# A decoder trunk's feed-forward scheme and rope: additions to h queued ahead of weight splits, and the queries' rotation in three operations

## The chip, the cores and the metric

One Trainium2 chip, of which the kernel uses one core. The time is that of one execution on the device in microseconds, the median of several executions. The profile is that of one execution; times in its rows count from the start of its span.

## The reference

A decoder trunk of two layers on 512 tokens of width 1024, all in float32. The first layer mixes with a state-space scan (Mamba-2), the second with latent attention whose keys and values come from one compressed projection; each layer ends with a gated feed-forward network (FFN) behind a depthwise convolution, and every residual sum is normalised.

```python
def conv_ffn(h, up, conv_w, conv_b, down):            # hidden width 2816
    u = causal_depthwise_conv(h @ up, conv_w, conv_b)
    g, val = jnp.split(u, 2, axis=-1)
    return (jax.nn.silu(g) * val) @ down

def apply_rope(x, cos, sin):                          # 64 per head, 8 heads
    x1, x2 = jnp.split(xf, 2, axis=-1)
    return jnp.concatenate([x1 * cos - x2 * sin, x2 * cos + x1 * sin], axis=-1)
...
    for i in range(DEPTH):
        mix = ssd_mixer(h, ...) if i < N_A_LAYERS else mla_attention(h, ...)
        h = layer_norm(DN_ALPHA * h + mix, ln_mix_g[i], ln_mix_b[i])
        ff = conv_ffn(h, ffn_up[i], ffn_conv_w[i], ffn_conv_b[i], ffn_down[i])
        h = layer_norm(DN_ALPHA * h + ff, ln_ffn_g[i], ln_ffn_b[i])
```

## The kernel before

**Precision.** Each float32 operand of a product is kept as two float32r parts, high and low, and each product is three matmuls (L154 to L156 in `mm_b`, L148 in `mm_a`): high by high, high by low, low by high.

**Weights.** `WStream` brings all weights in one sequence of tiles (128 x 1024 or less). For each tile there are four steps: SyncE issues the load into a staging buffer `wst` (three buffers), ACT casts it into the high part `wh` (L84), VectorE subtracts for the low part `wl` (L85), which frees the staging buffer for the next load, and TensorE uses the pair, after which the pair (six of them) is free again. ACT and VectorE together are called the split here. `ahead` splits as many tiles as buffers and a look-ahead of four allow; `get` calls it before each use, and the code calls it again where a product ends.

**The seven-product scheme.** Of the FFN's 22 rows of hidden channels the first 10 go through `down_pairs`: in place of eight block products (two token halves, two row parities, two output halves) it forms seven, of sums and differences of the operands. In order: a11, s1, s2 and s4 alternating, s3, a12, a22. Each has three weight tiles (1024, 1024 and 512 wide), and each works on two banks of PSUM: X[0] and X[1] (X), Y or Z. X is accumulated on in a11, s2, s3 and a22 (`start` is false after the first), so each time X must be added to h (`add`, L341, one operation for each bank) before the next product that uses it starts on that bank. The order of the additions in the code is X after a11, Y after s1, X and Y after s2/s4, X after s3, Z after a12, X after a22.

The operands on the weight side are sums too. Three buffers `rs` hold them: the first weights come by plain loads, s1's are made by an accumulating transfer that GpSimd issues (L57), s2's by VectorE's sum L78, s3's by VectorE's subtraction L81 into the staging buffer, a22's again by an accumulating transfer, which may start once L81 has read the sums.

**Who sets the order.** Engines work in order. The tile framework's scheduler fixes each engine's order when the kernel is built, from the order in the code and its own model of when operands are ready; SyncE's order alone is that of the code. `tc.issue_after(x)` puts what is issued inside it behind instruction x.

**Rope.** In the attention layer `rope` rotates 64 columns of each query head (four token tiles, 128 x 512 in PSUM, from `qr_tile`) and of the shared key (four tiles, 128 x 64, from `down`) into SBUF by six VectorE operations of half the width, L1029 to L1034. The rotated queries `qr` are transposed by TensorE (L1166), cast and split (`qrT`, L1170 and L1171) and used in the scores (L1183).

Of the kernel before, what the change touches and what calls it, by code (L numbers as in the profile page):

```python
# [9 lines left out]
F32 = mybir.dt.float32  # L10
# [4 lines left out]
ALU = mybir.AluOpType  # L15
# [3 lines left out]
P = 128  # L19
# [6 lines left out]
ALPHA = 4.0 ** 0.25  # L26
# [4 lines left out]
class WStream:  # L31
# [284 lines left out]
def down_pairs(k, ws, n, prs):  # L316

    nc = k.nc
    X, Y, Z = ([k.bank() for _ in range(2)] for _ in range(3))
    ni = (len(prs) + 1) // 2
    seen = set()

    def product(bs, op, p, i, start, stop):
        wh, wl = ws.get(i)
        ps = prs[2 * p:2 * p + 2]
        for t in range(2):
            for q, pr in enumerate(ps):  # L330
                x, c0 = pr[op]
                sl = slice(q * 512, (q + 1) * 512)
                k.mm_b(bs[t], x, slice(c0 + t * P, c0 + (t + 1) * P), wh[:, sl], wl[:, sl],
                       start and p == 0 and q == 0, stop and p == ni - 1 and q == len(ps) - 1)
        ws.retire(i)

    def add(bs, row, hf, sign):
        for t in range(2):
            i = 2 * row + t
            hs = k.h[:, i, hf * 512:(hf + 1) * 512]  # L340
            nc.vector.scalar_tensor_tensor(hs, hs, 1.0 if (i, hf) in seen else ALPHA, bs[t], op0=ALU.mult,  # L341
                                           op1=ALU.add if sign > 0 else ALU.subtract)
            seen.add((i, hf))

    for p in range(ni):
        product(X, "a11", p, n + p, True, True)
    n += ni
    ws.ahead(n)
    add(X, 0, 0, 1)
    for p in range(ni):  # L350
        product(Y, "s1", p, n + p, True, True)
    n += ni
    ws.ahead(n)
    add(Y, 1, 1, 1)
    for p in range(ni):
        product(X, "s2", p, n + 2 * p, False, True)
        product(Y, "s4", p, n + 2 * p + 1, False, True)
    n += 2 * ni
    ws.ahead(n)
    add(X, 0, 1, -1)  # L360
    add(Y, 0, 1, 1)
    for bs, op, s0, out in ((X, "s3", False, (1, 1, -1)), (Z, "a12", True, (0, 0, 1)), (X, "a22", False, (1, 0, 1))):
        for p in range(ni):
            product(bs, op, p, n + p, s0, True)
        n += ni
        ws.ahead(n)
        add(bs, *out)
    return n


def ffn(k, ws, base, cwp, gb, la=2, out=None, mid=None):

    nc, tc = k.nc, k.tc
    with ExitStack() as c:
# [10 lines left out]
        for r in range(2):  # L385
# [582 lines left out]
AH, QR, KVR, RD = 8, 384, 256, 64  # L968
# [49 lines left out]
    k.cs = cs  # L1018


def rope(k, dst, ps, i, nh, tmp):

    nc = k.nc
    cos = k.cs[:, 0, i, :].unsqueeze(1).broadcast_to([P, nh, 32])
    sin = k.cs[:, 1, i, :].unsqueeze(1).broadcast_to([P, nh, 32])
    x1, x2 = ps[:, :, 0:32], ps[:, :, 32:64]
    d1, d2 = dst[:, :, 0:32], dst[:, :, 32:64]
    t = tmp[:, :, 0:32]
    nc.vector.tensor_tensor(d1, x1, cos, op=ALU.mult)  # L1029
    nc.vector.tensor_tensor(t, x2, sin, op=ALU.mult)  # L1030
    nc.vector.tensor_tensor(d1, d1, t, op=ALU.subtract)
    nc.vector.tensor_tensor(d2, x2, cos, op=ALU.mult)
    nc.vector.tensor_tensor(t, x1, sin, op=ALU.mult)
    nc.vector.tensor_tensor(d2, d2, t, op=ALU.add)  # L1034


def mla(k, ws, base, ngp, gb):
    nc, tc = k.nc, k.tc
    with ExitStack() as cx:
        pool = lambda n, b, **kw: cx.enter_context(tc.tile_pool(name=n, bufs=b, **kw))  # L1040
        one = pool("a1", 1)
# [17 lines left out]
        qr = one.tile([P, NT, AH * RD], F32, name="qr")  # L1059
        n = [base]  # L1060
        tok = {}

        def down(i):
            bq, bk = k.bank(), k.bank()
# [19 lines left out]
            t = one.tile([P, 768], F32, name="ctok", tag=f"PT{i % 2}")  # L1084
# [278 lines left out]
```

## Time and profile before

| | |
|---|---|
| time, median of 3 runs | 1346.21 us (1342.25 to 1346.51) |
| the profiled execution | 1346.1 us, span 1344.4 us |
| TensorE busy | 1322.7 us, 98% |
| VectorE busy | 947.0 us, 70% |
| ACT busy | 618.0 us, 46% |
| GpSimd busy | 84.2 us, 6% |
| mean granted clock of TensorE | 0.993 |

In the rows PE is TensorE's matmul, PEld its weight load, DVE VectorE, POOL GpSimd, SPq SyncE's queue. A row names the line, the operation, output<-input by the program's names, partitions x elements, and how often (x). `[4.82 <-DVE h L341]` means that the engine stood idle 4.82 us until that work was done. PEclk is the clock that TensorE was granted, 1.00 being full speed.

### The profile page before, as it was taken

How to read it: one execution, taken by the hardware profiler on the slowest of the kernel's cores; microseconds unless marked ns; L12 is line 12 of the kernel's file. 1: busy time of each engine (PE TensorE's matmuls, PEld its weight loads, DVE VectorE, ACT ScalarE, POOL GpSimd, SP SyncE). 2: the span in 40 equal slices, each digit the busy share in tenths (PEclk: the TensorE clock that was granted, in tenths of full speed). 3: DMA queues.
4: the chain of work that ended last, by engine and by line, in shares of the span. 5: the costliest groups of instructions: out<-in, count | busy, mean ns of one | idle time of the engine just before them, and what ended most of it. 6: DMA issues, size and time to landing. Idle time of an engine off the chain costs nothing.

```text
span 1344.4 us, 17375 instructions
## 1 busy us (share of the span) xinstructions
PE 1322.7 (98%) x6794; PEld 1116.2 (83%) x6794; DVE 947.0 (70%) x1453; ACT 618.0 (46%) x988; POOL 84.2 (6%) x82
## 2 busy tenths in 40 slices
PE   9999999999999999899999999999999998999997
PEld 8888888888888888788888898888898886888886
DVE  6788898778798877756564366988576785565634
ACT  5765546545543544334443144664254443444411
POOL 0111001101102001000000021000100100000001
PEclk9999999999999999999999999999999998999999
DMA  7533432332331442542333222311143425432311
GB/s 241 178 108 110 126 111 78 110 125 79 110 101 47 152 137 48 139 167 95 95 98 105 63 89 65 93 48 65 34 161 103 120 65 159 144 95 95 100 56 63
DMA packets 47186, 140.39 MB, mean 104 GB/s; under 512 B 4960, under 2 KB 5984, under 8 KB 45568
## 3 DMA queue, kind: packets, MB, share of 16 engines
q1 hardware_dynamic: 44352, 134.04, 30.5%
q0 software_dynamic: 2752, 5.24, 2.4%
q8 instruction: 53, 0.87, 0.3%
q14 instruction: 29, 0.24, 0.1%
HBM read 137.10 MB, written 2.16 MB: 104 GB/s over the span
## 4 chain that ended last, share of the span: by engine, by line
PE 91%; DVE 4%; DMA 3%; ACT 1%; issue 1%; POOL 1%; SPq 0%; DVEq 0%; ACTq 0%; POOLq 0%
PE ps L148 56%; PE ps L154 9%; PE ps L156 9%; PE ps L155 9%; PE ps L1183 2%; DMA wst<-in_down_dram 1%; PE ps L729 1%; PE ps L1217 1%; PE ps L737 1%; DVE wl L85 1%; PE ps L234 1%; PE ps L1204 1%; PE ps L718 1%; PE ps L696 1%; PE ps L837 1%
## 5 line engine op out<-in xcount | busy, mean ns | idle before, releaser
L148 PE MATMUL ps<-ht,wh 128*128 128x512 f32 (+1 forms) x2272 | 518.7, 378 | 0.7 <-ACT ht L237 0.4
L148 PEld LDWEIGHTS ps<-ht,wh 128*128 128x128 f32 x2272 | 408.9, 188 | 80.0 <-ACT ht L237 0.8
L85 DVE TENSOR_TENSOR wl<-wst,wh 128x1024 fp32r<-128x1024 f32 (+3 forms) x220 | 259.1, 1182 | 108.0 <-ACT wh L84 107.5
L84 ACT CAST wh<-wst 128x1024 fp32r<-128x1024 f32 (+3 forms) x220 | 222.8, 1018 | 169.8 <-PE ps L156 92.4
L148 PE MATMUL ps<-ht,wl 128*128 128x512 f32 (+1 forms) x1136 | 267.3, 377 | 0.0
L148 PEld LDWEIGHTS ps<-ht,wl 128*128 128x128 f32 x1136 | 205.9, 188 | 39.5
L154 PE MATMUL ps<-wh,gt 128*128 128x512 f32 (+1 forms) x344 | 133.7, 389 | 9.6 <-DVE h L341 9.6
L155 PE MATMUL ps<-wl,gt 128*128 128x512 f32 (+1 forms) x344 | 132.9, 386 | 0.0
L156 PE MATMUL ps<-wh,gt 128*128 128x512 f32 (+1 forms) x344 | 132.8, 387 | 0.0
L283 DVE SCALAR_TENSOR_TENSOR acc<-ps,cw,acc 128x511 f32<-128x511 f32 x88 | 65.7, 746 | 88.6 <-ACT acc L282 88.6
L585 DVE SCALAR_TENSOR_TENSOR cv<-ps,cw,cv 128x511 f32<-128x511 f32 (+2 forms) x96 | 71.2, 744 | 34.0 <-ACT cv L583 33.4
L282 ACT ACTIVATE acc<-ps,cw 128x512 f32<-128x512 f32 x88 | 68.5, 778 | 36.8 <-PE ps L148 36.8
L154 PEld LDWEIGHTS ps<-wh,gt 128*128 128x128 f32 x344 | 65.7, 191 | 23.1 <-DVE h L341 10.5
L295 ACT CAST gt<-acc 128x512 fp32r<-128x512 f32 (+1 forms) x64 | 36.7, 586 | 96.9 <-DVE acc L288 96.0
L156 PEld LDWEIGHTS ps<-wh,gt 128*128 128x128 f32 x344 | 66.0, 192 | 13.2
L155 PEld LDWEIGHTS ps<-wl,gt 128*128 128x128 f32 x344 | 65.8, 191 | 12.8
L284 DVE SCALAR_TENSOR_TENSOR acc<-ps,cw,acc 128x510 f32<-128x510 f32 x88 | 65.8, 748 | 2.7
L287 ACT ACTIVATE acc<-acc 128x512 f32<-128x512 f32 x44 | 27.8, 632 | 82.6 <-DVE acc L284 82.3
L296 DVE TENSOR_TENSOR gt<-acc,gt 128x512 fp32r<-128x512 f32 (+1 forms) x64 | 40.7, 646 | 18.9 <-ACT gt L295 18.9
L688 ACT ACTIVATE W<-W,cum 128x128 f32<-128x128 f32 x128 | 41.1, 392 | 23.2 <-DMA W<-cumd 23.2
L154 PE MATMUL ps<-wh,yT 128*128 128x512 f32 x128 | 50.8, 397 | 0.0
L156 PE MATMUL ps<-wh,yT 128*128 128x512 f32 x128 | 49.9, 390 | 0.0
(242 smaller groups left out, 1624.3 us busy)
## 6 DMA issues: line engine op xcount, KB each, us to landing
wst<-in_up_dram SPq DMA_DIRECT2D x88, 512.0 KB, 3.4
wst<-in_down_dram SPq DMA_DIRECT2D x36, 512.0 KB, 3.5
wst<-in_xbc_dram SPq DMA_DIRECT2D x32, 512.0 KB, 3.9
W<-cumd SPq DMA_DIRECT2D x8, 1024.0 KB, 4.7
wst<-in_sow_dram SPq DMA_DIRECT2D x16, 512.0 KB, 3.5
wst<-in_zw_dram SPq DMA_DIRECT2D x14, 512.0 KB, 3.6
lngb<-in_gb_dram SPq DMA_DIRECT2D x4, 1024.0 KB, 7.0
rs<-in_down_dram POOLq DMA_DIRECT2D x8, 512.0 KB, 5.9
```

The source lines that it names most:

```text
L84: nc.scalar.copy(h[:, :f], s[:, :f])
L85: nc.vector.tensor_tensor(l[:, :f], s[:, :f], h[:, :f], op=ALU.subtract)
L148: nc.tensor.matmul(out, w[:, k, :], xts[k][:, x, ts], start=first and p == 0 and k == 0, stop=last and p == 2 and k == nk - 1, skip_group_ ...
L154: nc.tensor.matmul(out, xt[:, 0, tsl], wh, start=start, stop=False, skip_group_check=True)
L155: nc.tensor.matmul(out, xt[:, 0, tsl], wl, start=False, stop=False, skip_group_check=True)
L156: nc.tensor.matmul(out, xt[:, 1, tsl], wh, start=False, stop=stop, skip_group_check=True)
L282: nc.scalar.activation(a, b, AF.Identity, bias=cw[:, ch, 3:4], scale=cw[:, ch, 2:3])
L283: nc.vector.scalar_tensor_tensor(a[:, 1:], b[:, :SEQ - 1], cw[:, ch, 1:2], a[:, 1:], op0=ALU.mult, op1=ALU.add)
L284: nc.vector.scalar_tensor_tensor(a[:, 2:], b[:, :SEQ - 2], cw[:, ch, 0:1], a[:, 2:], op0=ALU.mult, op1=ALU.add)
L296: k.nc.vector.tensor_tensor(dst[:, 1, :], src, dst[:, 0, :], op=ALU.subtract)
L585: nc.vector.scalar_tensor_tensor(t[:, d:], b[:, :SEQ - d], cw[:, ch, 3 - d:4 - d], t[:, d:], op0=ALU.mult, op1=ALU.add)
L688: nc.scalar.activation(w, w, AF.Relu, bias=D["cum"][:, c, g * HPG + h:g * HPG + h + 1], scale=-1.0)
```

## The change

Two parts. In `down_pairs` each call of `ws.ahead` at a product's end now comes after the additions, and what it issues is put behind the last of them; after s2/s4 one such call comes after both pairs of additions. In `rope` the six operations become four: two products with sin into a scratch tile (the first negated), one product with cos over both halves at once, and one sum over the whole width, which for the queries GpSimd does. The scratch tile of the queries is twice as wide and alternates between two buffers.

```diff
-            nc.vector.scalar_tensor_tensor(hs, hs, 1.0 if (i, hf) in seen else ALPHA, bs[t], op0=ALU.mult,
-                                           op1=ALU.add if sign > 0 else ALU.subtract)
+            last = nc.vector.scalar_tensor_tensor(hs, hs, 1.0 if (i, hf) in seen else ALPHA, bs[t], op0=ALU.mult,
+                                                  op1=ALU.add if sign > 0 else ALU.subtract)
             seen.add((i, hf))
+        return last
+
+    def ahead(n, ins):
+
+        with k.tc.issue_after(ins.ins):
+            ws.ahead(n)
...
     n += ni
-    ws.ahead(n)
-    add(X, 0, 0, 1)
+    ahead(n, add(X, 0, 0, 1))
...
     n += 2 * ni
-    ws.ahead(n)
     add(X, 0, 1, -1)
-    add(Y, 0, 1, 1)
+    ahead(n, add(Y, 0, 1, 1))
...
-        ws.ahead(n)
-        add(bs, *out)
+        ahead(n, add(bs, *out))
...
-    nc.vector.tensor_tensor(d1, x1, cos, op=ALU.mult)
-    nc.vector.tensor_tensor(t, x2, sin, op=ALU.mult)
-    nc.vector.tensor_tensor(d1, d1, t, op=ALU.subtract)
-    nc.vector.tensor_tensor(d2, x2, cos, op=ALU.mult)
-    nc.vector.tensor_tensor(t, x1, sin, op=ALU.mult)
-    nc.vector.tensor_tensor(d2, d2, t, op=ALU.add)
+    halves = lambda t: t.rearrange("p h (a d) -> p (h a) d", a=2)
+    nc.vector.scalar_tensor_tensor(tmp[:, :, 0:32], ps[:, :, 32:64], -1.0, sin, op0=ALU.mult, op1=ALU.mult)
+    nc.vector.tensor_tensor(tmp[:, :, 32:64], ps[:, :, 0:32], sin, op=ALU.mult)
+    nc.vector.tensor_tensor(halves(dst), halves(ps), cos, op=ALU.mult)
+    add.tensor_tensor(dst, dst, tmp, op=ALU.add)
...
-            tmp = one.tile([P, AH, 32], F32, name="rtmp", tag="E1")
-            rope(k, qr[:, i].rearrange("p (h d) -> p h d", h=AH), b.rearrange("p (h d) -> p h d", h=AH), i, AH, tmp)
+            tmp = one.tile([P, AH, RD], F32, name="rtmp", tag=("E3", "PT2")[i % 2])
+            rope(k, qr[:, i].rearrange("p (h d) -> p h d", h=AH), b.rearrange("p (h d) -> p h d", h=AH), i, AH, tmp, nc.gpsimd)
```

VectorE's order in the first FFN, between s2/s4 and s3, before. ps_4851 and ps_4852 are X[0] and X[1], ps_4853 and ps_4854 Y; wst_4991, wst_5010 and wst_5029 are a12's three tiles.

```order
L85 TENSOR_TENSOR wl_5026<-wst_4972,wh_5025 128x512
L341 SCALAR_TENSOR_TENSOR h_93<-h_93,ps_4851 128x512
L85 TENSOR_TENSOR wl_5038<-wst_4991,wh_5037 128x1024
L85 TENSOR_TENSOR wl_5049<-wst_5010,wh_5048 128x1024
L341 SCALAR_TENSOR_TENSOR h_93<-h_93,ps_4852 128x512
L341 SCALAR_TENSOR_TENSOR h_93<-h_93,ps_4853 128x512
L341 SCALAR_TENSOR_TENSOR h_93<-h_93,ps_4854 128x512
L85 TENSOR_TENSOR wl_5070<-wst_5029,wh_5069 128x512
```

The same place in the changed kernel.

```order
L85 TENSOR_TENSOR wl_5026<-wst_4972,wh_5025 128x512
L341 SCALAR_TENSOR_TENSOR h_93<-h_93,ps_4851 128x512
L85 TENSOR_TENSOR wl_5038<-wst_4991,wh_5037 128x1024
L341 SCALAR_TENSOR_TENSOR h_93<-h_93,ps_4852 128x512
L341 SCALAR_TENSOR_TENSOR h_93<-h_93,ps_4853 128x512
L341 SCALAR_TENSOR_TENSOR h_93<-h_93,ps_4854 128x512
L85 TENSOR_TENSOR wl_5053<-wst_5010,wh_5052 128x1024
L85 TENSOR_TENSOR wl_5070<-wst_5029,wh_5069 128x512
```

a12's second tile (wst_5010) has moved from between X's two additions to behind all four; its first tile (wst_4991) has stayed between them.

VectorE's order in the same FFN from X's first addition to the split of s4's third tile, before. rs_3893 and rs2_3894 are the sums; wst_4902 is the staging buffer of s2's and s4's third tiles, wst_4939 and wst_4952 hold s3's first two.

```order
L341 SCALAR_TENSOR_TENSOR h_93<-h_93,ps_4851 128x512
L296 TENSOR_TENSOR gt_4815<-acc_4821,gt_4815 128x512
L296 TENSOR_TENSOR gt_4816<-acc_4822,gt_4816 128x512
L341 SCALAR_TENSOR_TENSOR h_93<-h_93,ps_4852 128x512
L85 TENSOR_TENSOR wl_4920<-rs_3893,wh_4919 128x1024
L85 TENSOR_TENSOR wl_4936<-wst_4873,wh_4935 128x1024
L85 TENSOR_TENSOR wl_4949<-rs2_3894,wh_4948 128x512
L341 SCALAR_TENSOR_TENSOR h_93<-h_93,ps_4853 128x512
L341 SCALAR_TENSOR_TENSOR h_93<-h_93,ps_4854 128x512
L85 TENSOR_TENSOR wl_4969<-wst_4902,wh_4968 128x512
L81 TENSOR_TENSOR wst_4939<-rs_3893,wst_4939 128x1024
L81 TENSOR_TENSOR wst_4952<-rs_3893,wst_4952 128x1024
```

The same stretch in the changed kernel, where the numbers wst_4904 and wst_4954 stand for wst_4902 and wst_4952.

```order
L341 SCALAR_TENSOR_TENSOR h_93<-h_93,ps_4851 128x512
L341 SCALAR_TENSOR_TENSOR h_93<-h_93,ps_4852 128x512
L85 TENSOR_TENSOR wl_4901<-wst_4749,wh_4900 128x1024
L85 TENSOR_TENSOR wl_4920<-rs_3893,wh_4919 128x1024
L85 TENSOR_TENSOR wl_4936<-wst_4873,wh_4935 128x1024
L341 SCALAR_TENSOR_TENSOR h_93<-h_93,ps_4853 128x512
L341 SCALAR_TENSOR_TENSOR h_93<-h_93,ps_4854 128x512
L78 TENSOR_TENSOR rs2_3894<-rs2_3894,wst_4904 128x512
L81 TENSOR_TENSOR wst_4939<-rs_3893,wst_4939 128x1024
L85 TENSOR_TENSOR wl_4951<-rs2_3894,wh_4950 128x512
L85 TENSOR_TENSOR wl_4969<-wst_4904,wh_4968 128x512
L81 TENSOR_TENSOR wst_4954<-rs_3893,wst_4954 128x1024
```

The additions stand in pairs. The sum L78 for s2's third tile, which before stood ahead of this stretch, and the first subtraction L81 now stand ahead of the splits of s2's and s4's third tiles (rs2_3894 and wst_4904). The second FFN's order is changed in the same way.

VectorE's order in the attention layer at the last query tile, before.

```order
L1125 TENSOR_TENSOR ht<-ps,ht 128x512 x3
L1029 TENSOR_TENSOR qr<-ps,cossin 128x8x32
L1030 TENSOR_TENSOR rtmp<-ps,cossin 128x256
L1032 TENSOR_TENSOR qr<-ps,cossin 128x8x32
L1031 TENSOR_TENSOR qr<-qr,rtmp 128x8x32
L85 TENSOR_TENSOR wl<-wst,wh 128x640
L1033 TENSOR_TENSOR rtmp<-ps,cossin 128x256
L85 TENSOR_TENSOR wl<-wst,wh 128x640
L1034 TENSOR_TENSOR qr<-qr,rtmp 128x8x32
```

The same place in the changed kernel; the sum of the query tile is GpSimd's (`L1032 TENSOR_TENSOR qr<-qr,rtmp 128x512 x4` there).

```order
L1123 TENSOR_TENSOR ht<-ps,ht 128x512 x3
L1029 SCALAR_TENSOR_TENSOR rtmp<-ps,cossin 128x8x32
L1030 TENSOR_TENSOR rtmp<-ps,cossin 128x8x32
L1031 TENSOR_TENSOR qr<-ps,cossin 128x512
L85 TENSOR_TENSOR wl<-wst,wh 128x640 x2
L1157 SCALAR_TENSOR_TENSOR qT<-ps,qT 128x512
L1157 SCALAR_TENSOR_TENSOR kT<-ps,kT 128x512
L85 TENSOR_TENSOR wl<-wst,wh 128x640
L1123 TENSOR_TENSOR ht<-ps,ht 128x512
```

Three of the tile's operations are gone from VectorE, and the splits of the heads' weights (L85) follow at once.

## Rows read from the trace of the kernel before

**Rows 1.** The page, busy time of each engine (share) and instructions.
```profile
PE 1322.7 (98%) x6794; PEld 1116.2 (83%) x6794; DVE 947.0 (70%) x1453; ACT 618.0 (46%) x988; POOL 84.2 (6%) x82
```
**Rows 2.** Waits of TensorE: total us, times, longest us.
```profile
PE ps L154 <- DVE h L341: 9.6, 2, 4.8
```
**Rows 3.** Chain of waits from 555 to 571: start, us, what.
```profile
557.74 9.31 DMA wst<-in_down_dram
```
**Rows 4.** Timeline of VectorE, both FFNs: start, us, line, operation [idle before].
```profile
551.02 0.68 DVE L85 TENSOR_TENSOR wl<-wst,wh 128x512 fp32r<-128x512 f32 x1
...
561.48 0.69 DVE L341 SCALAR_TENSOR_TENSOR h<-h,ps 128x512 f32<-128x512 f32 x1 [2.01 <-PE ps L156]
562.90 1.23 DVE L85 TENSOR_TENSOR wl<-wst,wh 128x1024 fp32r<-128x1024 f32 x1 [0.73 <-ACT wh L84]
568.24 1.23 DVE L85 TENSOR_TENSOR wl<-wst,wh 128x1024 fp32r<-128x1024 f32 x1 [4.11 <-ACT wh L84]
569.38 1.88 DVE L341 SCALAR_TENSOR_TENSOR h<-h,ps 128x512 f32<-128x512 f32 x3
...
1112.86 1.23 DVE L85 TENSOR_TENSOR wl<-wst,wh 128x1024 fp32r<-128x1024 f32 x1 [1.26 <-ACT wh L84]
```
**Rows 5.** Timeline of TensorE: matmuls 1, 128, 129, 210; 128, 210 of the second FFN.
```profile
536.12 0.39 PE L154 MATMUL ps<-wh,gt 128*128 128x512 f32 x1
...
564.91 0.39 PE L155 MATMUL ps<-wl,gt 128*128 128x512 f32 x1
570.11 0.79 PE L154 MATMUL ps<-wh,gt 128*128 128x512 f32 x1 [4.82 <-DVE h L341]
...
590.93 0.39 PE L156 MATMUL ps<-wh,gt 128*128 128x512 f32 x1
...
1114.33 0.39 PE L155 MATMUL ps<-wl,gt 128*128 128x512 f32 x1
...
1140.37 0.39 PE L156 MATMUL ps<-wh,gt 128*128 128x512 f32 x1
```
**Rows 6.** Windows: us, PE, PEld, DVE, ACT, POOL busy, PEclk, DMA share, GB/s.
```profile
536.12:564.90 28.78, 28.78 (x128) 23.84 (x127) 22.56 (x30) 12.41 (x16) 3.30 (x3) 1.00 0.48 120
564.90:575.25 10.35, 5.53 (x14) 4.03 (x13) 4.67 (x6) 2.61 (x3) 0.00 (x0) 0.67 0.59 203
```
**Rows 7.** Transfers issued from 551.5 to 557: count, KB each, us to landing.
```profile
wst<-in_down_dram SPq DMA_DIRECT2D x1, 256.0 KB, 2.6
...
wst<-in_down_dram SPq DMA_DIRECT2D x1, 512.0 KB, 6.4
...
rs<-in_down_dram POOLq DMA_DIRECT2D x1, 256.0 KB, 10.4
```
**Rows 8.** Windows, the stretch from 556 to 568; columns as in rows 6.
```profile
556.00:568.00 12.00, 9.30 (x42) 7.35 (x40) 3.83 (x4) 2.98 (x4) 0.89 (x1) 1.00 1.01 256
```
**Rows 9.** Waits of TensorE between 820 and 870.
```profile
PE ps L156 <- DVE cT L1108: 0.6, 1, 0.6
PE ps L1183 <- DVE qrT L1171: 0.5, 1, 0.5
PE ps L1166 <- DVE qr L1034: 0.3, 1, 0.3
```
**Rows 10.** Windows, the stretch with the waits for qr and qrT.
```profile
844.00:852.00 8.00, 7.17 (x40) 6.03 (x40) 7.47 (x15) 5.85 (x10) 0.00 (x0) 1.00 0.36 97
```
**Rows 11.** Groups of VectorE, 829 to 850: busy us, mean ns, idle before.
```profile
L1125 DVE TENSOR_TENSOR ht<-ps,ht 128x512 fp32r<-128x512 f32 x7 | 4.6, 682 | 0.0
...
L1029 DVE TENSOR_TENSOR qr<-ps,cossin 128x256 f32<-128x256 f32 x4 | 1.7, 419 | 0.0
```
**Rows 12.** Timelines of GpSimd and VectorE in the scan of the first layer.
```profile
125.88 3.54 POOL L684 TENSOR_TENSOR CE<-CE,cv 128x1536 f32<-128x1536 f32 x1 [34.10 <-ACT CE L683]
...
125.96 4.01 DVE L744 SCALAR_TENSOR_TENSOR cv<-cv,zs 128x512 f32<-128x512 f32 x1
```
**Rows 13.** Timeline of TensorE: the last query tile's last matmul, the last transpose.
```profile
841.10 0.39 PE L156 MATMUL ps<-wh,cT 128*128 128x512 f32 x1
...
846.90 0.33 PE L1166 MATMUL ps<-ident,qr 128*128 128x128 f32 x1 [0.32 <-DVE qr L1034]
```

More of the change, by code (lines that the diff above doesn't have):

```diff
@@ L352, in down_pairs @@
     n += ni
-    ws.ahead(n)
-    add(Y, 1, 1, 1)
+    ahead(n, add(Y, 1, 1, 1))
     for p in range(ni):
@@ L365, in down_pairs @@
         n += ni
-        ws.ahead(n)
-        add(bs, *out)
+        ahead(n, add(bs, *out))
     return n
@@ L1018, in rope_tables, with rope @@
     k.cs = cs
-def rope(k, dst, ps, i, nh, tmp):
+def rope(k, dst, ps, i, nh, tmp, add):
     nc = k.nc
-    cos = k.cs[:, 0, i, :].unsqueeze(1).broadcast_to([P, nh, 32])
+    cos = k.cs[:, 0, i, :].unsqueeze(1).broadcast_to([P, 2 * nh, 32])
     sin = k.cs[:, 1, i, :].unsqueeze(1).broadcast_to([P, nh, 32])
-    x1, x2 = ps[:, :, 0:32], ps[:, :, 32:64]
-    d1, d2 = dst[:, :, 0:32], dst[:, :, 32:64]
-    t = tmp[:, :, 0:32]
-    nc.vector.tensor_tensor(d1, x1, cos, op=ALU.mult)
-    nc.vector.tensor_tensor(t, x2, sin, op=ALU.mult)
-    nc.vector.tensor_tensor(d1, d1, t, op=ALU.subtract)
-    nc.vector.tensor_tensor(d2, x2, cos, op=ALU.mult)
-    nc.vector.tensor_tensor(t, x1, sin, op=ALU.mult)
-    nc.vector.tensor_tensor(d2, d2, t, op=ALU.add)
+    halves = lambda t: t.rearrange("p h (a d) -> p (h a) d", a=2)
[3 more added lines that the diff above has]
+    add.tensor_tensor(dst, dst, tmp, op=ALU.add)
 def mla(k, ws, base, ngp, gb):
@@ L1093, in down @@
             kr = t[:, QR + KVR:].rearrange("p (a d) -> p a d", a=2)
-            tmp = one.tile([P, AH, 32], F32, name="rtmp", tag="E1")
-            rope(k, kr[:, 0:1], bk[:, KVR:KVR + RD].unsqueeze(1), i, 1, tmp[:, 0:1])
+            tmp = one.tile([P, 1, RD], F32, name="ktmp", tag="E1")
+            rope(k, kr[:, 0:1], bk[:, KVR:KVR + RD].unsqueeze(1), i, 1, tmp, nc.vector)
             nc.vector.tensor_copy(kr[:, 1], kr[:, 0])
@@ L1133, in qr_tile @@
                 k.mm_b(b, cT[kk], slice(i * P, (i + 1) * P), w[kk // 2][0][:, o:o + 512], w[kk // 2][1][:, o:o + 512], kk == 0, kk == 2)
-            tmp = one.tile([P, AH, 32], F32, name="rtmp", tag="E1")
-            rope(k, qr[:, i].rearrange("p (h d) -> p h d", h=AH), b.rearrange("p (h d) -> p h d", h=AH), i, AH, tmp)
+            tmp = one.tile([P, AH, RD], F32, name="rtmp", tag=("E3", "PT2")[i % 2])
+            rope(k, qr[:, i].rearrange("p (h d) -> p h d", h=AH), b.rearrange("p (h d) -> p h d", h=AH), i, AH, tmp, nc.gpsimd)
         for i in range(NT):
```

## The prediction

> **What bounds the kernel now.** I read the page first: TensorE is busy for nearly the whole span [rows 1], so a change wins only where TensorE waits or runs at its lower clock. Its list of waits then shows one that counts: the first matmul of `mm_b` waits for an addition to h, twice, 9.6 us together [rows 2], once in each FFN, in the seven-product scheme. The chain of waits says why the addition is late: a load of a down weight needs 9.31 us to land [rows 3], ACT's cast and VectorE's split of that tile follow, and only then comes the addition. VectorE works in order. At the first place it starts the addition of X[0] at 561.48, then two splits of a12's tiles, the second at 568.24 after an idle time of 4.11, since that tile had not landed; X[1]'s addition stands behind it and starts at 569.38 [rows 4]. s3 accumulates on in X[1], so its matmul there starts only at 570.11 [rows 5].
>
> The wait is not its whole price. The scheme has 210 matmuls (5 pairs x 7 products x 2 banks x 3). The first 128 start from 536.12 to 564.91 [rows 5], one every 28.79 / 127 = 0.2267 us, at granted clock 1.00; over the next ten microseconds the mean is 0.67 [rows 6], since after the idle time the clock is at the lower of its levels, 1.2 instead of 2.4 GHz, for a while. At the first pace the 82 matmuls that are left take 82 x 0.2267 = 18.59 us; the last starts at 590.93, 26.02 us after the 128th [rows 5]. The place loses 7.43 us: 4.97 of waiting (570.11 against 565.14) and 2.46 of slow matmuls. The second place loses 1140.37 - 1114.33 - 18.59 = 7.45 [rows 5]. **14.9 us** can be had here.
>
> **The change, part by part.** (1) *Additions ahead of the splits.* No operation is added. Of the two splits between X[0]'s and X[1]'s addition the second, whose tile is late, moves behind all four additions; the first stays. X[1]'s new start follows from that first split: it starts at 562.90, the next operation after one of its size starts 1.14 later (568.24 to 569.38 [rows 4]), so the addition runs from 564.04 and takes 0.69, and its matmul follows within 0.04, at 564.77. Without the stall that matmul, the 127th, is due at 536.12 + 126 x 0.2267 = 564.68: 0.1 us is left. At the second place the first split starts at 1112.86 [rows 4], so the matmul can start at 1114.73; it is due one step before the 128th, at 1114.11 [rows 5]: 0.6 us is left.
>
> What is late next? The split that moves back holds a12's second tile, wanted by matmul 163 at 536.12 + 162 x 0.2267 = 572.85; it ended at 568.24 + 1.23 = 569.47 [rows 4], 3.4 us early. a22's splits and the loads of the next round wait for matmuls to release buffers, and move forward with TensorE.
>
> (2) *The scheme's early part is reordered too, and with it a load.* The first additions to X and Y come as pairs now; X is ready after 30 matmuls, 542.9, and next wanted at matmul 61, 549.72: this costs nothing. But the sum L78 for s2's third tile now stands behind Y's additions, and a long subtraction (L81) ahead of the splits of s2's and s4's third tiles. The last of these used to run from 551.02 to 551.70 [rows 4]; its end let s3's third tile be loaded, 256 KB in 2.6 us [rows 7]. In the new order Y's second addition can start when matmul 60 is through, at about 549.9; it takes 0.6, then L78 0.6, L81 1.14 and two splits 0.6 each: the last ends at about 553.5, 1.8 us later than before. So the load falls into the burst of a22's accumulating transfers. From 556 to 568 the transfer engines are full, at 256 GB/s [rows 8]; a 512 KB load issued at 555.35 took 6.4 us [rows 7]. s3's third tile itself is wanted only by matmul 145, at 568.8. But 256 KB at 256 GB/s are 1.0 us by which the next load, a12's first tile, can be held back, and X[1]'s addition stands behind that tile's split. Bounds at each place: 0, if they land before the burst is full, and 1.0; I take 0.5, since the load is issued about when the burst begins. With 0.1 and 0.6 from above, **1.7 us** of the 14.9 stay, between 0 and 2.7. Waits of this length leave the clock alone: where TensorE waits for qr and qrT [rows 9] the granted clock stays 1.00 [rows 10].
>
> (3) *Rope.* For each of four query tiles six VectorE operations of 256 elements, 0.33 from start to start, become two of these and one of 512, 0.60 from start to start (0.42 and 0.68 long [rows 11]): 2.0 becomes 1.27, and VectorE gains 0.73 x 4 = 2.9 us. The last sum goes to GpSimd, where no row has its size: 1536 elements take 3.54 us [rows 12], so 512 take 1.18, an estimate by size, bounded below by VectorE's 0.68 and above by the whole 3.54. Ahead of the heads TensorE waits 0.3 for qr and 0.5 for qrT [rows 9], as VectorE is late there. The last query tile's matmuls start until 841.10 [rows 13]: three operations from 841.6 end at 842.9, GpSimd's sum at 844.1, or 846.5 at its upper bound; the transposes that take it start at 846.1, and the last of them stood ready for 0.32 us when it started at 846.90 [rows 13]. So both waits go, **-0.8 us**, and with the 0.1 that each key tile saves VectorE, once on the path, -0.9; between -1.4 (the 0.6 before cT [rows 9] gone too) and +1.8 (below).
>
> Against this stands a pair of rows: VectorE's L744, 512 elements in SBUF, started 0.08 us after GpSimd's multiplication, took 4.01 and ended after it [rows 12], where the addition of the same size takes 0.69 [rows 4]. So one engine can lock the other out. The Trainium skill (SBUF — State Buffer, Who interferes with whom) has the rule: a VectorE instruction with both inputs in SBUF and a GpSimd instruction that reads SBUF exclude each other for a whole instruction, whichever starts first. By that rule, the trace agrees. Around the new sums VectorE mostly reads PSUM and one SBUF operand; only behind the fourth tile stand splits, which read two. If each of the four sums held VectorE for 1.18 it would lose 4.7 and gain 2.9: +1.8.
>
> **The sum.** -14.9 + 1.7 - 0.9 = -14.1 us. The profiled execution took 1346.1, practically the median of 1346.2: **1332.0 us**.
>
> **Rivals.** *B: a12's first tile comes later than I take*, the reordered loads sharing the burst worse, by 1.5 to 3 us at each place. X[1]'s addition and TensorE wait that long, and if the clock falls, another 2.46: 1332.0 + 2 x (1.5 to 5.5 - 0.5) = 1334 to 1342. For it: loads of the burst took 6.4 and 9.3 us [rows 3, 7]. Against it: this load is issued only about 0.5 us later than before. *C: rope costs*, +1.8 in place of -0.9: 1334.7. Against it: one of the four sums has such operations beside it. *D: slower.* s3's third tile, now loaded in the burst, lands only when the whole burst is in, as the 256 KB of its last accumulating transfer did, 10.4 us after issue at 556.5 [rows 7]: 566.9, and 1.0 more for the bytes that it adds. VectorE would wait for it at a subtraction (L81) ahead of all four additions: 567.9 + 0.6 + 1.14 + 0.6 starts X[0]'s addition at 570.2, and matmul 121, due at 563.3, at 570.95. That is 7.6 of waiting and 2.46 of slow matmuls for 7.43 now, twice: 1346.1 + 5.3 - 0.9 = 1350.5. It decides from a landing after about 565. Against it: the load of 555.35 came after 6.4 us in the same burst, which here would be 560. *E: nothing moves*, since weights are late as soon as additions are not: 1345.2. a12's second tile has 3.4 us of room and would have to come 8.4 later to eat all.
>
> **Chances.** Forecast 0.76 (its own range 1329.8, every wait of the first two parts gone, to 1335), B 0.13, C 0.04, E 0.04, D 0.03. To leave out no more than 2 in 10 the range goes from 1329.3 to 1337.5, which takes in C and the lower half of B. About 0.3%, 4 us, is what a measurement of this kernel tells from no change (the three runs span 4.3 us): faster 0.93, within 0.3% 0.04, slower 0.03.
>
> **What would show it.** In the changed profile TensorE waits for h nowhere longer than 1.5 us, and the granted clock of the 210 matmuls is 1.00 throughout, so that they start within 47.4 to 49 us instead of 54.8. X[1]'s addition starts right behind one split. The load of s3's third tile takes longer than 2.6 us. The waits for qr and qrT are gone and GpSimd's sums take about 1.2 us. I am wrong if a wait of 2 us or more stands at s3, or if the clock still falls there.

## The result: 0.73% faster, the forecast number held, its term for the load did not

The changed kernel takes 1333.66 us in the median of 6 runs (1332.25 to 1337.48); the kernel before takes 1344.7 in 6 runs (1342.25 to 1346.51). The ratio is 0.9927, with a 95% interval of 0.9912 to 0.9942. Forecast were 1332.0, between 1329.3 and 1337.5, and 0.93 for faster by over 0.3%. As a ratio, though, 1332.0 to 1346.1 is 0.9895, outside the interval: the forecast gain of 14.1 us was too large beside the 11.0 between the medians. The two profiled executions, 1346.1 and 1332.25, differ by 13.85.

The changed kernel's list of TensorE's waits (total us, times, longest) answers to [rows 2, 9]:

```profile
PE ps L154 <- DVE h L341: 2.6, 2, 1.4
...
PE ps L1181 <- DVE qrT L1169: 0.4, 1, 0.4
```

Its timeline of TensorE, with the first matmul of the scheme, the first of s3 and the last, in the first FFN and then in the second, answers to [rows 5]:

```profile
535.85 0.39 PE L154 MATMUL ps<-wh,gt 128*128 128x512 f32 x1
...
565.92 0.50 PE L154 MATMUL ps<-wh,gt 128*128 128x512 f32 x1 [1.35 <-DVE h L341]
...
584.91 0.39 PE L156 MATMUL ps<-wh,gt 128*128 128x512 f32 x1
...
1077.62 0.39 PE L154 MATMUL ps<-wh,gt 128*128 128x512 f32 x1
...
1107.61 0.50 PE L154 MATMUL ps<-wh,gt 128*128 128x512 f32 x1 [1.27 <-DVE h L341]
...
1126.56 0.39 PE L156 MATMUL ps<-wh,gt 128*128 128x512 f32 x1
```

The 210 matmuls now start within 584.91 - 535.85 = 49.06 and 48.94 us, where it was 54.81 and 54.82. Two windows around the waits that are left (columns as in rows 6) show the granted clock at 1.00, TensorE's full 2.4 GHz:

```profile
562.80:575.00 12.20, 10.85 (x48) 8.63 (x47) 9.09 (x11) 5.79 (x7) 0.00 (x0) 1.00 0.69 220
1102.00:1115.00 13.00, 11.73 (x53) 9.38 (x51) 7.97 (x11) 5.14 (x6) 0.00 (x0) 1.00 0.77 219
```

VectorE's timeline in the first FFN shows what is left, and answers to [rows 4]:

```profile
561.21 0.69 DVE L341 SCALAR_TENSOR_TENSOR h<-h,ps 128x512 f32<-128x512 f32 x1 [1.67 <-PE ps L156]
564.05 1.23 DVE L85 TENSOR_TENSOR wl<-wst,wh 128x1024 fp32r<-128x1024 f32 x1 [2.15 <-ACT wh L84]
565.19 1.88 DVE L341 SCALAR_TENSOR_TENSOR h<-h,ps 128x512 f32<-128x512 f32 x3
```

X[1]'s addition stands right behind the split of a12's first tile, as the order said. But that split starts 564.05 - 535.85 = 28.20 us after the scheme's first matmul, where it was 562.90 - 536.12 = 26.78 [rows 4, 5]. Its tile comes later. The issues of s3's third tile and of a12's first, timeline of SyncE's queue:

```profile
553.31 0.34 SPq L65 DMA_DIRECT2D wst<-in_down_dram  x1
...
555.58 0.37 SPq L65 DMA_DIRECT2D wst<-in_down_dram  x1
```

and, from the list of transfers, their size and the time from issue to landing [rows 7]:

```profile
wst<-in_down_dram SPq DMA_DIRECT2D x1, 256.0 KB, 3.7
...
wst<-in_down_dram SPq DMA_DIRECT2D x1, 512.0 KB, 7.3
```

Counted from the scheme's first matmul, a12's first tile was issued at 19.23 and took 6.4; now it is issued at 19.73 and takes 7.3. That is 0.5 and 0.9 us, the 1.4 by which the split is late. (In the second FFN it starts 28.11 us after the first matmul instead of 27.31.) The issue is later because it follows VectorE's split of s3's first tile, which frees the staging buffer: that split starts 554.33 - 535.85 = 18.48 us after the first matmul, where it was 554.10 - 536.12 = 17.98, since the sum L78 and one split more now stand between Y's additions and it.

All profiles can be cut at four matmuls, the first and the last of either scheme. The table gives the starts' distances in us; the stretch from the second scheme's last matmul to the end is 204.0 in every one, and the first scheme starts at 534.8 to 536.1. The kernels below the third profile of the changed one are the experiments of the next section.

| profile | first scheme | between (holds rope) | second scheme | time of that execution |
|---|---|---|---|---|
| before | 54.81 | 494.62 | 54.82 | 1346.1 |
| before again | 54.15 | 493.29 | 55.35 | 1344.0 |
| changed | 49.06 | 492.71 | 48.94 | 1332.25 |
| changed again | 48.99 | 493.46 | 51.69 | 1335.65 |
| changed, third | 48.92 | 493.42 | 49.93 | 1333.5 |
| scheme only | 48.97 | 493.12 | 48.89 | 1331.6 |
| load early, again | 47.65 | 493.29 | 47.61 | 1329.3 |
| rope only | 54.04 | 492.71 | 55.99 | 1343.7 |
| split behind | 47.38 | 492.71 | 47.37 | 1328.6 |
| load early | 47.37 | 493.53 | 47.38 | 1329.2 |
| split behind, old rope | 47.38 | 493.16 | 47.38 | 1329.2 |
| split behind, sum on VectorE | 47.37 | 492.60 | 47.38 | 1327.8 |
| before, filled | 52.28 | 492.95 | 53.50 | 1339.4 |
| changed, filled | 49.38 | 492.70 | 49.90 | 1333.0 |

At an even pace of 0.2267 the 210 matmuls need 209 x 0.2267 = 47.38 us, and four kernels reach that.

### The profile page after: what moved, and what is told of

The parts are those of the page before. It is cut to its first block, busy times and chain, and to the rows that moved or that the text cites. A ratio compares the mean times of both kernels' runs of the same rounds, so it can differ in the third digit from the quotient of the medians.

```text
span 1330.5 us, 17374 instructions
## 1 busy us (share of the span) xinstructions
PE 1317.7 (99%) x6794; PEld 1114.5 (84%) x6794; DVE 945.3 (71%) x1433; ACT 616.7 (46%) x988; POOL 88.9 (7%) x86
## 4 chain that ended last, share of the span: by engine, by line
PE 95%; DVE 2%; DMA 2%; issue 1%; ACT 0%; SPq 0%; DVEq 0%; ACTq 0%
PE ps L148 57%; PE ps L154 9%; PE ps L156 9%; PE ps L155 9%; PE ps L1181 2%; PE ps L731 1%; PE ps L1215 1%; DMA wst<-in_down_dram 1%; PE ps L739 1%; DVE wl L85 1%; PE ps L234 1%; PE ps L720 1%; PE ps L698 1%; PE ps L1202 1%; PE ps L839 1%; PE ps L672 1%
## 5 line engine op out<-in xcount | busy, mean ns | idle before, releaser
L85 DVE TENSOR_TENSOR wl<-wst,wh 128x1024 fp32r<-128x1024 f32 (+3 forms) x220 | 259.8, 1188 | 99.0 <-ACT wh L84 98.7
L154 PE MATMUL ps<-wh,gt 128*128 128x512 f32 (+1 forms) x344 | 131.8, 383 | 2.6 <-DVE h L341 2.6
L156 PE MATMUL ps<-wh,gt 128*128 128x512 f32 (+1 forms) x344 | 131.4, 382 | 0.0
L154 PE MATMUL ps<-wh,yT 128*128 128x512 f32 x128 | 50.9, 397 | 0.0
L686 POOL TENSOR_TENSOR CE<-CE,cv 128x1536 f32<-128x1536 f32 x8 | 28.6, 3575 | 326.2 <-ACT CE L685 326.2
```

The costliest lines, as they stand in the source:

```text
L85: nc.vector.tensor_tensor(l[:, :f], s[:, :f], h[:, :f], op=ALU.subtract)
L154: nc.tensor.matmul(out, xt[:, 0, tsl], wh, start=start, stop=False, skip_group_check=True)
L156: nc.tensor.matmul(out, xt[:, 1, tsl], wh, start=False, stop=stop, skip_group_check=True)
```

## The experiments

The theory: the gain is the wait for h and the slow matmuls behind it; what is left is a12's first tile, late by a shifted load; rope is worth about 0.9 us. The rivals: rope carries more, or costs; the slow matmuls or the spread of the times have another source; the shifted load plays no part.

**Each part alone** (*scheme only*, *rope only*). The one keeps the new `down_pairs` and puts the old rope back; the other is the reverse.

```diff
# scheme only: the changed kernel, with
-    add.tensor_tensor(dst, dst, tmp, op=ALU.add)
+    nc.vector.tensor_tensor(d1, x1, cos, op=ALU.mult)
...
# rope only: the changed kernel, with
-    ahead(n, add(X, 0, 0, 1))
+    ws.ahead(n)
+    add(X, 0, 0, 1)
...
```

> The reordered additions and splits alone, rope as before. Theory (the gain is the wait for h and the slow matmuls behind it, rope is worth about 0.9): 0.5 to 1.5 us slower than the changed kernel, near 1334.5, ratio to before about 0.993; the waits of TensorE for h are 2.6 us in all, as in the changed kernel, and those for cT, qr and qrT stand as before (1.4 in all). Rival (rope costs by the lock-out between VectorE and GpSimd): 0.5 to 2 us faster than the changed kernel. Rival (rope carries a good part of the gain): 1337 or more.

> Rope in three operations with GpSimd's sum alone, additions and splits as before. Theory: 0.5 to 1.5 us faster than before (ratio 0.9990 to 0.9996, hardly to be told from 1), waits of TensorE for h as before (about 9.6 us), those for cT, qr and qrT down from 1.6 to about 0.6. Rival (lock-out costs): 1 to 2 us slower than before, ratio above 1.0005. Rival (rope carries much): 3 us or more faster.

Scheme only: 1333.64 (1331.64 to 1338.04), ratio 0.9926 [0.9910, 0.9942], the changed kernel's own 0.9927. Rope only: 1343.18 beside 1343.41, ratio 0.9996 [0.9987, 1.0004]. The whole measurable gain is the scheme's; rope alone can't be told from nothing, and scheme only is no slower than the changed kernel, where 0.5 to 1.5 us were expected. In the scheme-only kernel the waits for cT and qr are gone as well, with the old rope (only 0.4 for qrT is left): against the expectation, and against the prediction's reading of them.

**The last split, and the load ahead of it** (*split behind*; *load early*). The first puts the split of a12's first tile behind all four additions and keeps the reordered early part. The second puts the ends of a11 and s1 back as they were, and leaves the rest as in the changed kernel.

```diff
# split behind: the changed kernel, with
-        wh, wl = ws.get(i)
+        wh, wl = ws.get(i, la)
...
-        product(Y, "s4", p, n + 2 * p + 1, False, True)
+        product(Y, "s4", p, n + 2 * p + 1, False, True, 3 if p == ni - 1 else None)
# load early: the changed kernel, with
-    ahead(n, add(X, 0, 0, 1))
+    ws.ahead(n)
+    add(X, 0, 0, 1)
...
-    ahead(n, add(Y, 1, 1, 1))
+    ws.ahead(n)
+    add(Y, 1, 1, 1)
```

> The changed kernel, with the split of a12's first tile behind all four additions too (it stood between X[0]'s and X[1]'s). Early part as in the changed kernel. Theory (the 1.35 and 1.27 us that are left at s3 are this split, which waits for its load): both waits are gone (under 0.2 each) and the kernel is 2.2 to 2.8 us faster than the changed one, near 1331 (ratio to before about 0.9905), and the 210 matmuls start within 47.5 us. Rival (what is late is X's or Y's own matmuls or VectorE's own work): waits for h of 0.6 us or more stay at both places. Rival (the split that moves back makes a12's weights late): a wait of TensorE for wl at a12 takes its place, and the time is that of the changed kernel.

> The changed kernel with the ends of a11 and s1 as before: the operations L78 and L81 stand again where they did, so that s3's third tile is loaded early; the split of a12's first tile stands behind all four additions, as in the run before this one. Theory: the load of s3's third tile (256 KB) takes 2.6 to 3.0 us again, a12's first tile lands about 1 us earlier than in the changed kernel, and as nothing on TensorE's path waits for that tile any more, the time is that of the run before this one within 0.5 us (near 1331), with both waits for h under 0.2. Rival (the reordered early part costs by itself, through the burst of a22's transfers): 1 us or more faster than the run before. Rival (it brings something by itself): 1 us or more slower.

The second expectation has the split behind the additions in that kernel too. The trace shows it elsewhere. VectorE's timeline in the first FFN, split behind and then load early:

```profile
560.78 2.73 DVE L341 SCALAR_TENSOR_TENSOR h<-h,ps 128x512 f32<-128x512 f32 x4 [1.60 <-PE ps L156]
563.64 1.23 DVE L85 TENSOR_TENSOR wl<-wst,wh 128x1024 fp32r<-128x1024 f32 x1
```

```profile
560.53 0.69 DVE L341 SCALAR_TENSOR_TENSOR h<-h,ps 128x512 f32<-128x512 f32 x1 [2.01 <-PE ps L156]
561.42 1.23 DVE L85 TENSOR_TENSOR wl<-wst,wh 128x1024 fp32r<-128x1024 f32 x1 [0.20 <-ACT wh L84]
562.56 1.87 DVE L341 SCALAR_TENSOR_TENSOR h<-h,ps 128x512 f32<-128x512 f32 x3
```

In load early the split stands between X[0]'s and X[1]'s additions, as in the changed kernel, and only the early part differs from that kernel. So the two runs each take one thing away, the split or the late load; no run takes away both.

Split behind: 1329.3 (1328.61 to 1329.48), ratio 0.9891 [0.9874, 0.9909]. Load early: 1329.19 (1329.01 to 1330.74), 0.9893 [0.9877, 0.9908]. No wait for h is left in either list, and no other takes its place; windows of the first kernel show TensorE busy throughout:

```profile
564.80:575.00 10.20, 10.20 (x47) 8.45 (x46) 7.18 (x9) 5.16 (x6) 0.00 (x0) 1.00 0.57 197
1102.00:1115.00 13.00, 13.00 (x59) 10.74 (x58) 9.15 (x12) 6.09 (x7) 0.00 (x0) 1.00 0.71 213
```

Both beat the changed kernel, by 4.4 us between medians, more than the 2.2 to 2.8 expected, and their times spread by 0.9 and 1.7 us (four executions each) instead of 5.2 (six). Either is enough: with the split behind, the load may stay late; with the load early, the split may stay between.

**What the reordered early part costs** (*load early, again*). The early part is as before, so that s3's third tile is loaded early, and the split of a12's first tile is held by the code between X[0]'s and X[1]'s additions. It stood there already in load early: the order of instructions is the same in the two traces on every engine, so this is one more execution of that order.

```diff
-    add(X, 0, 1, -1)
-    ahead(n, add(Y, 0, 1, 1))
+    x0 = add(X, 0, 1, -1, [0])
+    if ws.sp < n + ni:
+        with k.tc.issue_after(x0.ins):
+            ws._split()
...
+    with k.tc.issue_after(ws.last.ins):
+        add(X, 0, 1, -1, [1])
+        y = add(Y, 0, 1, 1)
+    ahead(n, y)
```

> The changed kernel with the early part of the scheme as before (s3's third tile loaded early) and the split of a12's first tile between X[0]'s and X[1]'s additions, as in the changed kernel. Theory of the prediction (of the 1.35 and 1.27 us left, about 0.5 each come from the load that the reordered early part shifts into a22's burst, the rest from the split as such): s3's third tile takes 2.6 to 3 us to load, a12's first tile lands about 1 us earlier, the waits for h are 0.1 to 0.9 us, and each scheme takes 47.5 to 48.4 us instead of 49.0. Rival (the shifted load plays no part; the tile's landing varies by itself): waits of 1.2 us or more and 48.9 us again.

One execution: 1329.31, and schemes of 47.65 and 47.61 us. Timeline of VectorE in the first FFN, and the two transfers:

```profile
560.42 0.69 DVE L342 SCALAR_TENSOR_TENSOR h<-h,ps 128x512 f32<-128x512 f32 x1 [2.01 <-PE ps L157]
561.87 1.22 DVE L85 TENSOR_TENSOR wl<-wst,wh 128x1024 fp32r<-128x1024 f32 x1 [0.76 <-ACT wh L84]
563.01 1.88 DVE L342 SCALAR_TENSOR_TENSOR h<-h,ps 128x512 f32<-128x512 f32 x3
```

```profile
wst<-in_down_dram SPq DMA_DIRECT2D x1, 256.0 KB, 2.5
...
wst<-in_down_dram SPq DMA_DIRECT2D x1, 512.0 KB, 6.4
```

The first matmul stands at 535.05, so X[1]'s addition starts 27.96 us after it; the prediction's part (1) had 564.04 - 536.12 = 27.92. In load early a12's first tile took 5.8 us to land instead of 6.4, and the addition starts at 562.56 - 535.17 = 27.39. The same split in the same place costs 0.27 and 0.23 us here (47.65 and 47.61 less 47.38) and nothing in load early, and 1.51 to 1.68 in the four schemes of the two profiles of around 1332. The other 1.3 to 1.7 us at each place is the reordered early part. The rival, that it plays no part, falls: the four schemes with the early part as before take 47.37 to 47.65 us, the eight of the changed kernel and scheme only 48.89 or more, and the five executions 1329.01 to 1330.74 us, where the eight of the changed kernel take 1332.25 or more.

What within the early part does it isn't separated. The load of s3's third tile is issued 1.8 us later and that of a12's first tile 0.5 later, but GpSimd's accumulating transfers beside them move too: the first is issued 0.5 us earlier (16.76 instead of 17.25 after the first matmul), the second 0.6 later (19.10 instead of 18.46).

**The price of the slow matmuls** (*before, filled*) **and the spread of the times** (*changed, filled*). Additional matmuls ahead of s3 keep TensorE busy while it would wait.

```diff
+    g = prs[0]["a22"][0]
+    for _ in range(21):
+        nc.tensor.matmul(Z[0], g[:, 0, 0:P], g[:, 0, :], start=True, stop=True, skip_group_check=True)
     add(X, 0, 1, -1)
```

The changed kernel gets 6 in place of 21.

> The kernel before, with 21 more matmuls of the scheme's size (128 rows, 512 columns, 21 x 0.2267 = 4.76 us) ahead of s3 in both FFNs, where TensorE waited for X[1]'s addition for 4.97 us. They write a bank that a12's first matmul starts anew, so nothing of the output changes; additions, splits and loads stand as before. Theory (of the 7.4 us lost at each place 2.46 are matmuls at the lower clock that the idle time brings): TensorE has no idle time long enough, the granted clock over the ten microseconds behind is 1.00 instead of 0.67, and the kernel is 4 to 5 us faster than before, ratio 0.9963 to 0.997, though the addition comes no earlier. Rival (the slow matmuls are slow for their operands or for VectorE's and ACT's traffic, not for the idle time): no faster, ratio 0.9995 to 1.001. Rival (the fillers hold back what follows): slower by up to 9.5 us.

> The changed kernel with 6 such matmuls (1.36 us) ahead of s3 in both FFNs, where it waited 1.35 and 1.27 us for X[1]'s addition. Theory (the times of the changed kernel spread from 1332.2 to 1337.5 since in some executions the clock falls at these waits, 2.46 us for each; the runs with those splits out of the way spread by 0.9): the waits are below 0.3 us, all times lie within 2 us of each other, near 1332, and the median is 1 to 2 us under the changed kernel's 1333.7. Rival (the spread has another source): times up to 1337 again. Rival (the fillers cost their own time): median 1334 or more.

Before, filled: 1339.35 (1339.13 to 1341.04) beside 1342.61, ratio 0.9977 [0.9967, 0.9986]: faster with 9.5 us more matmuls, at a mean granted clock of 0.999 over the whole program, where the runs of before beside it had 0.993 to 0.997. At the first place the scheme takes 52.28 = 47.38 + 4.76 of fillers + 0.14; that is 2.53 less than 54.81, against 2.46 read from that trace for the slow matmuls. The price varies: over the six places profiled with the old order (before, before again, rope only) the slow matmuls (what the scheme takes beyond 47.38 and the wait) cost 1.7 to 3.0 us. At the second place a wait stays, which is part of why the whole came to 3.3 and not to 4 or 5:

```profile
1114.73 0.50 PE L154 MATMUL ps<-wh,gt 128*128 128x512 f32 x1 [1.02 <-DVE h L341]
```

Changed, filled: 1332.98, with all five times between 1332.27 and 1333.72. None of the five is long, as expected. The median fell by 0.7 only, under the 1 to 2 expected, and the ratio to before, 0.9927 [0.9914, 0.9939], not at all, as waits of 0.3 and 0.9 stayed behind the fillers (X[1]'s addition came later again) and the bound of 0.3 was missed.

**The spread seen directly.** The changed kernel and the kernel before were profiled again, with no edit.

> The changed kernel once more, for another profile. Theory (in some executions the clock falls at the waits that are left at s3): where the time is 1332 to 1333 the granted clock is 1.00 over both FFNs' schemes and their 210 matmuls start within 49 us each; where it is 1334 or more, one or both of these stretches is 1.5 to 2.5 us longer, at a granted clock below 1.00 in the ten microseconds behind the wait. Rival (the time varies elsewhere, at the program's start or around the heads): both schemes take 49 us whatever the time.

> As the run before this one: the changed kernel a third time. Theory: a time of 1334 or more goes with a scheme stretch longer than 49 us and a granted clock below 1.00 behind its wait for h. Rival: with a longer stretch elsewhere.

> The kernel before once more, for another profile. In its first profile (1346.1) the two schemes took 54.81 and 54.82 us and the stretch between them 494.62, while the runs with rope as before and other schemes had 492.95 to 493.16 there. Theory (that profile was taken at a high time of the kernel before, 1.5 us of it in the stretch between, where TensorE waited 0.6 for cT): the stretch between takes about 493.1 and the time is 1342 to 1345, the two schemes together 108 to 110.5. Rival (rope in six operations costs the 1.9 us always): 494.6 again.

The second profile of the changed kernel was of a long execution, 1335.65. Rows of its TensorE timeline at s3 of the second FFN, then windows over the idle time and behind it:

```profile
1109.35 0.50 PE L154 MATMUL ps<-wh,gt 128*128 128x512 f32 x1 [2.37 <-DVE h L341]
...
1110.23 0.63 PE L154 MATMUL ps<-wh,gt 128*128 128x512 f32 x1
1110.65 0.63 PE L155 MATMUL ps<-wl,gt 128*128 128x512 f32 x1
```

```profile
1106.98:1109.35 2.37, 0.01 (x1) 0.01 (x1) 1.88 (x3) 0.46 (x1) 0.00 (x0) 1.00 0.84 273
1109.35:1113.60 4.25, 4.25 (x12) 3.33 (x13) 3.42 (x5) 2.60 (x3) 0.00 (x0) 0.60 0.42 130
1110.20:1113.40 3.20, 3.20 (x9) 2.50 (x8) 2.37 (x4) 2.60 (x3) 0.00 (x0) 0.50 0.38 147
```

TensorE had been idle for 2.37 us, and its granted clock had a mean of 0.60 over the next 4.25; from 1110.20 to 1113.40 it was 0.50, the lower level of 1.2 GHz, and the matmuls start 0.42 apart instead of 0.23. The scheme takes 51.69. In the third profile the same wait is 2.25 long, but the matmuls behind it keep the full clock:

```profile
1102.00:1115.00 13.00, 10.74 (x48) 8.58 (x47) 7.69 (x10) 4.97 (x6) 0.00 (x0) 1.00 0.78 222
```

Its scheme takes 49.93. So a12's first tile lands with a lateness that varies (in the second FFN its transfer took 8.3 us in the long execution and 8.2 in the third profile, 7.2 in the first), and the clock sometimes falls on top of it, for another 1.6 (51.69 - 49.93, less 0.12 of wait). The expectation, 1.5 to 2.5 more in one stretch at a clock below 1.00, came out in the second profile with 2.7 more; in the third the stretch between the schemes gave 0.7 as well, which it had not foreseen. Of the 8 executions of the changed kernel 3 took more than 1334.5, of the 16 of kernels without any wait for h at s3 (split behind, load early and the two rope kernels at the end of this section) none took more than 1330.74. The mean granted clock of whole executions goes with the time: 0.996 and 0.997 in the timed ones of 1337.48 and 1334.92, 0.998 or 0.999 in the other four.

The kernel before, a second time, took 1344.01, with 493.29 between its schemes. So 494.62 was that one execution's, as the theory had it. In the second profile TensorE waits 0.5 for qrT, and neither for cT nor for qr. Matmul by matmul, the first profile loses its 1.3 us in that stretch at just these places: 0.9 at the wait for cT and 0.5 at that for qr, 0.1 at that for qrT, less 0.2 behind it. So waits with rows of 0.63 and 0.32 us of idle time cost 0.9 and 0.5.

**Rope beside a quiet scheme** (*split behind, old rope*; *split behind, sum on VectorE*). Both are the kernel of 1329.3, whose times spread least.

```diff
# old rope: the kernel with the split behind, with
-    add.tensor_tensor(dst, dst, tmp, op=ALU.add)
+    nc.vector.tensor_tensor(d1, x1, cos, op=ALU.mult)
...
# sum on VectorE: the kernel with the split behind, with
-            rope(k, qr[:, i].rearrange("p (h d) -> p h d", h=AH), b.rearrange("p (h d) -> p h d", h=AH), i, AH, tmp, nc.gpsimd)
+            rope(k, qr[:, i].rearrange("p (h d) -> p h d", h=AH), b.rearrange("p (h d) -> p h d", h=AH), i, AH, tmp, nc.vector)
```

> The kernel with the split of a12's first tile behind all four additions (median 1329.3, times within 0.9), with rope in six operations on VectorE as before. Theory (rope is worth what TensorE waits less for qr, qrT and cT, 0.4 to 1.9 by the four profiles so far): 0.4 to 1.9 us slower, 1329.7 to 1331.2. Rival (the lock-out costs as much as the shorter rope gains): the same within 0.3, or faster.

> The same kernel (split behind, 1329.3) with rope in three operations and the sum, but the sum on VectorE too. VectorE has four operations of 0.68 more, and no operation of GpSimd beside it. Theory (TensorE waits for the last query's transposes only; a sum of 0.68 behind its queue against 1.29 on an idle engine comes out even): within 0.6 us of 1329.3. Rival (the lock-out on VectorE is what GpSimd's sums cost): 1 us or more faster. Rival (VectorE's queue is what makes qr late): 0.7 us or more slower, with waits for qr back.

Old rope: 1329.51 (1329.04 to 1330.32), ratio 0.9902 [0.9888, 0.9915], beside the new rope's 1329.3 and 0.9891 [0.9874, 0.9909]. That is 0.2 us slower by the medians and 1.5 by the ratios, as the two were timed beside different executions of before (medians 1342.6 and 1343.4). The intervals overlap: neither the 0.4 to 1.9 expected nor its rival is decided. Sum on VectorE: 1328.5 (1327.83 to 1330.33), ratio 0.9898 [0.9883, 0.9913]: 0.8 us faster than 1329.3 by the medians and 0.9 slower by the ratios. These runs can't tell it from even, nor do they fix it within the 0.6 expected. The lock-out can be seen in the rows, but not told in the time. The changed kernel's timelines of GpSimd (the third and fourth sum) and of VectorE beside the fourth:

```profile
830.05 1.29 POOL L1032 TENSOR_TENSOR qr<-qr,rtmp 128x512 f32<-128x512 f32 x1 [1.16 <-DVE qr L1031]
836.08 1.80 POOL L1032 TENSOR_TENSOR qr<-qr,rtmp 128x512 f32<-128x512 f32 x1 [4.74 <-DVE qr L1031]
```

```profile
835.92 2.65 DVE L85 TENSOR_TENSOR wl<-wst,wh 128x640 fp32r<-128x640 f32 x2
```

and VectorE's timeline of the kernel with the sum on VectorE:

```profile
833.53 0.82 DVE L85 TENSOR_TENSOR wl<-wst,wh 128x640 fp32r<-128x640 f32 x1
834.26 0.69 DVE L1032 TENSOR_TENSOR qr<-qr,rtmp 128x512 f32<-128x512 f32 x1
834.86 0.83 DVE L85 TENSOR_TENSOR wl<-wst,wh 128x640 fp32r<-128x640 f32 x1
```

Two splits that take 0.82 each take 2.65 beside GpSimd's sum, 1.0 too long, and the sum takes 1.80 instead of 1.29. The second split ends at 838.57, 0.69 behind the sum's end at 837.88, as if it had waited for the whole sum. The prediction's rule (the Trainium skill, SBUF — State Buffer, Who interferes with whom) speaks of this, and the trace agrees.

## Why the prediction was right, and where it was off

**The place and the mechanism** held: the waits for h and the slow matmuls behind them were what the scheme lost, X[1]'s addition moved behind one split, and the whole measurable gain is there (scheme only, rope only). The clock's part, 2.46 of 7.43 in that profile, was measured by itself: 2.53 at the first place of the kernel before, filled. The split that moved back made nothing late, so rival E is out. Rival D is out too: s3's third tile landed after 3.7 us.

**Part (1), what the split itself leaves**: forecast 0.1 and 0.6, measured 0.27 and 0.23 in one execution with the load early and nothing in the other. (X[1]'s first matmul is the 127th in the changed kernel's order, as the prediction took it; in the kernel before two others went ahead, so that its wait stands at the 129th.)

**Part (2) was mis-sized: the load.** The load of s3's third tile is issued 553.31 - 535.85 = 17.46 us after the scheme's first matmul, and 15.62 with the early part as before: the forecast 1.8 later. The part priced the shifted load by bytes, 0 to 1.0 us at each place, and took 0.5. Measured were 1.3 to 1.7 for the reordered early part. In the first FFN two things add up: the transfer of a12's first tile takes 0.9 longer, inside the bounds, and it is also issued 0.5 later, which the text knew (it stands under rival B, as evidence against it) and never put into the sum. So 1.68 + 1.56 = 3.2 us stay at s3 in the profiled execution, not 1.7 and above the bound of 2.7. The part also said that waits of this length leave the clock alone, from rows with waits of 0.3 and 0.5. That is true of 1.35, 1.27 and, once, 2.25, and not of the 2.37 of a longer execution. That is rival B, which had 0.13: in its mechanism and price it happened in part of the executions (1335.65 lies in its 1334 to 1342), and the median lies just below it. Two cases with chances of their own were here two faces of one kernel.

**Part (3) rests on waits that don't always stand there: rope.** Its -0.9 came from the waits for qr and qrT, and its bound of -1.4 from that for cT, in one execution (with the 0.1 of the key tiles the bound would be -1.5). In the second profile of before and in the scheme-only kernel, both with the old rope, the waits for cT and qr are absent; the new rope has some of them back (0.3 and 0.4 for cT in the second and third profile). Between the schemes the old rope has 492.95 to 493.29 but for the first profile, the new one 492.70 to 493.53. By the times it is worth nothing (scheme only beside the changed kernel), 0.2 to 0.5 us (rope only, by median and ratio) or 0.2 to 1.5 (old rope behind the split): neither the 0.9 nor none is ruled out. Rival C, that it costs 1.8, is: the interval of rope only ends at 1.0004, 0.5 us.

**The sum.** The two profiled executions differ by 13.85, near the forecast 14.1, but by errors that cancel: the schemes gave 109.63 - 98.00 = 11.6 where 13.2 were forecast, and the stretch between them 1.9 where 0.9 was, most of that a mark of the execution of before (0.3 lies ahead of the first scheme). Between the medians it is 11.0: 1346.1 was a high time to start from (the medians of before were 1344.7, 1343.4 and 1342.6 in three comparisons), and 1332.25 was the lowest of the changed kernel's.

**What was to show it** came out so in the first profile (no wait over 1.5, clock 1.00, three of the four sums of 1.3 us), with three near misses: 49.06 where 49 was the limit, 0.4 of the wait for qrT left, and the fourth sum of 1.80. By its own words (wrong with a wait of 2 us or more at s3, or with a falling clock there) it is wrong of the second and third profile.

What stays open: which of the early part's shifts makes a12's first tile land later, what makes its landing vary from one execution to the next, and what rope is worth.

## What to carry to other kernels

When a reordering removes a stall, ask what its new order delays: here the reordered early part issued one load 1.8 us later and the next 0.5 later, and that next one, on which the same addition still depended, landed 1.4 us later. Price both effects, later issue and slower transfer. Better, leave the early part alone or take the last dependence away: either made the kernel faster by another 4.4 us and its times steadier. Read the order that an edit makes from its trace before arguing from it, since a split meant to stand behind the additions stood between them. And read the small waits, of a few tenths, in two profiles before a sum is built on them: those for cT and qr came and went between executions.

## What the runs showed of the hardware

An idle time of TensorE of 2.25 us left its granted clock at 1.00, one of 2.37 us at the same place of another execution brought it to a mean of 0.60 over the next 4.25, 0.50 in most of it. Doing useless work can so be cheaper than waiting: 42 added matmuls, 9.5 us of TensorE's time, made the kernel before 3.3 us faster. The wait that the change leaves was 1.2 to 2.4 us long in three profiles. It mostly costs its own length and 0.3 us more (1.68 for 1.35), but in its longest case it brought a second price, 1.6 us of slow matmuls. Its times spread by 5 us, those without it by 1 to 2.5.
